# Rotary embedding of q and k as one 512-column tile, and low-order terms multiplied last, in a two-layer decoder trunk

## The chip, the cores and the metric

The kernel runs on one core of a Trainium2 chip. A core has a matrix engine (TensorE, "PE" in the profile, whose weight loads "PEld" run beside its matmuls), a vector engine (VectorE, "DVE"), a scalar engine (ScalarE, "ACT"), a general engine (GpSimd, "POOL") and a queue that issues transfers (SyncE, "SP"). The metric is the time of one execution in microseconds. Before the change it is 579.99 us, the median of three runs (579.93 to 580.3).

## The reference

The input is 256 tokens of 1024 numbers in fp32. Two layers follow one another. Layer 0 mixes tokens with 16 attention heads of 64; it is a block-sparse attention with blocks of 256 tokens, and as there are only 256 tokens, each query sees just its own block, so it is plain causal attention. Layer 1 has 12 heads in three groups, with dilated windows (128 wide with step 1, 512 with step 4, 2048 with step 16), merged over the groups by their softmax denominators. After each mixer comes a normalisation, then a squared-ReLU MLP (1024 to 4096 to 1024) and another normalisation. Cut to what matters:

```python
def apply_rotary(t, cos, sin):            # on q and on k, every head
    t1, t2 = jnp.split(t, 2, axis=-1)
    return jnp.concatenate([t1 * c - t2 * s, t2 * c + t1 * s], axis=-1)
...
x = layer_norm(alpha * x + mixer(x))      # q, k, v = x @ w_qkv; rotary; softmax(q k^T / 8) v; @ w_o
x = layer_norm(alpha * x + relu(x @ w_in) ** 2 @ w_out)
```

## The kernel before

**Numbers in two parts.** Each fp32 operand is split into a high part in a 4-byte matmul type (fp32r) and the rest: `split` makes `hi` as an ACT copy (L309) and `lo` as a DVE subtract (L314). A product is three matmul terms: hi by hi, lo by hi, hi by lo. Weights come in tiles of 128x1024: `load_w` issues one transfer of 512 KB into one of four `raw` buffers, ACT writes `whi`, DVE writes `wlo`; there are ten slots for each. `xs` holds the two parts of the layer's input with features on the partitions, in eight slices of 128 features (`kt`, 0 to 7).

**Matmuls.** Three helpers record them. `mm_wstat` (L440) has the weights stationary and makes a 128x256 tile of q or k (two heads by 256 tokens): for each `kt`, hi by hi, hi by lo part of x, lo weight by hi, 24 matmuls of 256 columns in all. `mm_xstat` (L466) has the input stationary and makes a 128-token half of V or of an MLP chunk kept in token order, 512 columns at a time, again with the three terms together for each `kt`. `mm_rows` multiplies an activation tile with a row block of an output weight (attention output or second MLP weight) into four accumulators. All matmuls go through one line, L318. PSUM has two families of banks of 128x512, four named `acc` and four named `tp`.

**Attention.** Heads are worked in pairs: eight in layer 0, six in layer 1. For a pair, `project` (or the step `qk` of layer 1) multiplies q, rotates q, multiplies k, rotates k. The feature order within a pair is laid out so that the two halves of the rotation lie 64 partitions apart. `rotate` (L511) does three DVE multiplies from PSUM with a table of cosines and sines (128x256 by cos into `a`; two of 64x256 by sin into `b`, each reading the other half's partitions), one POOL add of 128x256 (L503), and then the split into `qhi` and `qlo`, or, for k, a split twice with a mask for each head (`khi` on ACT, L529; `klo` on DVE, L508). `score` makes the scores from those, `softmax` masks (DVE, L563), takes exponentials (ACT, L573) and scales (DVE, L580); then the probabilities are transposed on PE (L587), copied out by ACT (`pt`, L595) and multiplied with V. The first four weight tiles of layer 0, two pairs, are interleaved with the loading of the input (`Stage`, `first_ps`): they have four `acc` banks, one for each of q0, k0, q1, k1.

**Seams.** At the end of a mixer or MLP, `out_and_ln` (L722) does the output products of token half 0, its normalisation (`ln_half`, L668: DVE sums and statistics, a POOL power, DVE scalings into `tok`, PE transposes of `tok`, and the split into `xs`), then those of half 1. Before the normalisation of half 1 a function `between` records the first work of the next stage that needs half 0 alone: `Mlp.head`, with `half(0)`, or layer 1's V for half 0 (`v1`). `TAIL` says how many of the last output row blocks are held back to be done bank by bank there; for layer 1's mixer it is 5 of 6. `half(m)` of the MLP makes one 512-wide chunk in token order: `mm_xstat`, then `relu_sq_tok` (ACT relu L749 and square L750 into `hrt`, four PE transposes, a split). The other seven chunks go through `mm_wstat_wide` and `relu_sq_T`.

**The order of the work.** The code above only records operations, with what they read and write, a cost and an engine. A planner (`Plan.order`) then gives each a due time, counted back from the PE operations that need it in recorded order, and builds one fixed order for each engine: at each step the operation that can start first, and of those the one with the smallest due time. PE's own due times come from the recorded order of stages, which is a string for each layer (`ORDER0`, `HEAD1`, `ORDER1`; `qk-p` projects a pair, `v` makes V, `s` is scores and softmax, `o` the product with V). SP issues the transfers in the order of recording. So a change of a recorded operation can move others on every engine.

Of the kernel before, what the change touches and what calls it, by code (L numbers as in the profile page):

```python
# [29 lines left out]
TAIL = (5, 5, 5, 8)  # L30
# [48 lines left out]
class Op:  # L79
    __slots__ = ("n", "eng", "cost", "fn", "preds", "succs", "bufs", "due", "wait", "ready", "end", "xfer", "early")  # L80


class Plan:
# [16 lines left out]
    def op(self, eng, cost, fn, reads=(), writes=(), xfer=0.0, early=0.0):  # L100
        o = Op()
        o.n, o.eng, o.cost, o.fn, o.xfer = len(self.ops), eng, cost, fn, xfer
        o.early = early
# [24 lines left out]
        self.ops.append(o)  # L128
        return o

    def order(self):
        clock = {e: BEGIN[e] for e in ("PE", "SP")}
        bus = 0.0
        for o in self.ops:
            t = max([clock.get(o.eng, 0.0)] + [p.end + latency(p, o) for p in o.preds])
            o.end = t + o.cost
            if o.eng in clock:
                clock[o.eng] = o.end
            if o.xfer:
                bus = o.end = max(t + FETCH, bus) + o.xfer  # L140
            o.due = t if o.eng == "PE" else None
# [101 lines left out]
    "bst mx sm mv rstd ta hrt raw whi wlo g b xs0 xs1 tok m1 ahi alo ropet khi klo v sc1 sc0 pt0 pt1 m0 qhi qlo ident"  # L243
# [5 lines left out]
def tile_trunk(  # L249
# [87 lines left out]
    class Stage:  # L337
# [40 lines left out]
        def mms(self, ps, j):  # L378
            kt, hi, lo = self.kt, self.hi, self.lo
            c = slice(self.col(j), self.col(j) + P)  # L380
            i = (kt, self.part(j))
            for w, p, start, stop in ((hi, 0, kt == 0, False), (hi, 1, False, False), (lo, 0, False, kt == KT - 1)):
                op(
                    "PE", 0.12,
                    lambda w=w, p=p, start=start, stop=stop: mm(
                        ps.t[:, :S], w.t[:, c], xs[kt // 4].t[:, kt % 4, p, :], start, stop
                    ),
                    [(w, i)] + [(xs[kt // 4], (p, kt, m)) for m in range(2)], [ps],
                )
# [18 lines left out]
    idle = mk([P, S], F32, "ta", 5)  # L408
    op("DVE", 0.1, lambda: nc.vector.memset(idle.t, 0.0), (), [idle])
    idle_ps = psum("tp")  # L410
    for _ in range(NWARM):
        op("PE", 0.43, lambda: mm(idle_ps.t[:, :S], idle.t[:, :P], idle.t, True, True), [idle], [idle_ps])
# [27 lines left out]
    def mm_wstat(ps, w):  # L440
        for kt in range(KT):

            def go(kt=kt):
                c = slice(kt * P, (kt + 1) * P)
                a, b = (xs[kt // 4].t[:, kt % 4, part, :] for part in range(2))
                first, last = kt == 0, kt == KT - 1
                mm(ps.t[:, :S], w.hi.t[:, c], a, first, False)
                mm(ps.t[:, :S], w.hi.t[:, c], b, False, False)
                mm(ps.t[:, :S], w.lo.t[:, c], a, False, last)

            op("PE", 0.36, go, [(w.hi, 0), (w.lo, 0)] + xk(kt, (0, 1)), [ps])
# [14 lines left out]
    def mm_xstat(ps, ws, m, n):  # L466
        t = slice(m * P, (m + 1) * P)
        for kt in range(KT):
            per = 1024 // n
            w = ws[kt // per]  # L470

            def go(kt=kt, w=w):
                c = slice((kt % per) * n, (kt % per + 1) * n)
                a, b = (xs[kt // 4].t[:, kt % 4, part, t] for part in range(2))
                mm(ps.t[:, :n], a, w.hi.t[:, c], kt == 0, False)
                mm(ps.t[:, :n], a, w.lo.t[:, c], False, False)
                mm(ps.t[:, :n], b, w.hi.t[:, c], False, kt == KT - 1)

            op("PE", 3 * (n / 2400 + 0.0135), go, [(w.hi, 0), (w.lo, 0)] + xk(kt, (m,)), [ps])
# [31 lines left out]
    def rotate(ps, kind, ropet):  # L511
        a = mk([P, S], F32, "ta", 5)
        b = mk([P, S], F32, "ta", 5)
        tt(S, lambda: a.t, lambda: ps.t[:, :S], lambda: ropet.t[:, 0, :], ALU.mult, [ps, ropet], [a],
           extra=0.1)
        tt(S, lambda: b.t[0:64, :], lambda: ps.t[64:128, :S], lambda: ropet.t[64:128, 1, :], ALU.mult,
           [ps, ropet], [(b, 0)], extra=0.1)
        tt(S, lambda: b.t[64:128, :], lambda: ps.t[0:64, :S], lambda: ropet.t[0:64, 1, :], ALU.mult,
           [ps, ropet], [(b, 1)], extra=0.1)
        tt(S, lambda: a.t, lambda: a.t, lambda: b.t, ALU.add, [a, b], [a], ADD_ENG)  # L520
        if kind == "q":
            hi, lo = mk([P, S], F32R, "qhi", 2), mk([P, S], F32R, "qlo", 2)
            split(S, lambda: a.t, lambda: hi.t, lambda: lo.t, [a], [hi], [lo], sbuf=True)
        else:
            hi, lo = mk([P, 2, S], F32R, "khi", 2), mk([P, 2, S], F32R, "klo", 2)
            for h in range(2):
                op(
                    "ACT", act(S, 1, True),
                    lambda h=h: nc.scalar.activation(hi.t[:, h, :], a.t, AF.Copy, scale=hm.t[:, h : h + 1]),  # L529
                    [a, hm], [(hi, h)],  # L530
                )
                stt(
                    S, 1, lambda h=h: lo.t[:, h, :], lambda: a.t, lambda h=h: hm.t[:, h : h + 1],
                    lambda h=h: f32(hi.t[:, h, :]), ALU.mult, ALU.subtract, [a, hm, (hi, h)], [(lo, h)],
                )
        return hi, lo

    def proj_qk(w):
        ps = psum("acc")
        mm_wstat(ps, w)  # L540
        return ps

    first_ps = [psum("acc") for _ in range(NFIRST)]
    for st in stages:
        for j, ps in enumerate(first_ps):
            st.mms(ps, j)
# [35 lines left out]
    def transposes(ps, pairs, r):  # L582
# [6 lines left out]
        op("PE", 0.109 * len(pairs), go, list(r) + [ident], [ps])  # L589
# [78 lines left out]
    def ln_half(pieces, m, gb, last):  # L668
# [21 lines left out]
        for n in range(2):  # L690
# [12 lines left out]
            if not last:  # L703
                ps = psum("tp")
                transposes(
                    ps, [(j * P, lambda k=n * 4 + j: z.t[:, k * P : (k + 1) * P]) for j in range(4)], [(z, n)]
# [15 lines left out]
    def out_and_ln(acc, items, ntail, gb, last, between):  # L722
# [4 lines left out]
        for m in range(2):  # L727
# [5 lines left out]
            ln_half(acc[m], m, gb, last)  # L733

    def relu_sq_T(ps, ahi, alo, j):
        u = mk([P, S], F32, "ta", 5)
        h = mk([P, S], F32, "ta", 5)
        keys = [(j, 0), (j, 1)]
        op("ACT", act(S), lambda: nc.scalar.activation(u.t, ps.t[:, S:], AF.Copy), [ps], [u])  # L739
        tt(S, lambda: u.t, lambda: ps.t[:, :S], lambda: u.t, ALU.add, [ps, u], [u])  # L740
        stt(S, 0, lambda: h.t, lambda: u.t, lambda: 0.0, lambda: u.t, ALU.max, ALU.mult, [u], [h])
        split(
            S, lambda: h.t, lambda: ahi.t[:, j, :], lambda: alo.t[:, j, :], [h],
# [3 lines left out]
    def relu_sq_tok(ps, m, ahi, alo):  # L747
        r = mk([P, 512], F32, "hrt", 1)
# [11 lines left out]
    class Mlp:  # L760
# [55 lines left out]
    def layer0(between):  # L816
# [3 lines left out]
        def do_v(n):  # L820
            ws = [load_w(wv0[n * 4 + j]) for j in range(4)]
            if n == 0:
                late["m0"] = const(mask0, [P, 256], "m0")
                late["ident"] = const(ident_in, [P, P], "ident")
            V[n] = []
            for m in range(2):
                ps = psum("tp" if n == m == 0 else "acc")
                mm_xstat(ps, ws, m, 512)
                V[n].append(evac_v(ps, 512))

        def softmax(q, k):
# [12 lines left out]
            m0 = late["m0"]  # L844
            for e, c, s, mc, i, n in regs:
                mask_min(
                    n, lambda e=e, c=c: e.t[:, c], lambda s=s, c=c: s.t[:, c], lambda mc=mc: m0.t[:, mc],
# [13 lines left out]
        def project(p):  # L861
            return [
                rotate(
                    first_ps[i] if i < NFIRST else proj_qk(load_w(wqk0[i - NFIRST])), kind,
                    ropes[0],
                )
                for i, kind in ((2 * p, "q"), (2 * p + 1, "k"))
            ]
# [26 lines left out]
    def v1(i, m):  # L895
# [4 lines left out]
        mm_xstat(ps, wv[i], m, v_cols[i])  # L900
# [6 lines left out]
    def layer1(between):  # L907
# [4 lines left out]
        for step, a in (x.split("-") for x in ORDER1.split()):  # L912
# [4 lines left out]
            if step == "qk":  # L917
                qk[u, gi] = [
                    rotate(proj_qk(load_w(wqk1[u * 6 + 2 * gi + i])), kind, ropes[1]) for i, kind in enumerate("qk")
                ]  # L920
# [68 lines left out]
def _layout(inputs):  # L989
# [48 lines left out]
    d["rope0"] = np.stack([np.concatenate([c] * 4), np.concatenate([s, s, -s, -s])], axis=1)  # L1038
# [48 lines left out]
```

## Time and profile before

| | value |
|---|---|
| median of 3 runs | 579.99 us (579.93 to 580.3) |
| the profiled execution | 579.34 us |
| its span in the trace | 577.2 us |
| mean granted TensorE clock | 0.996 |
| PE busy | 562.7 us, 97% |
| DVE busy | 431.3 us, 75% |
| ACT busy | 299.9 us, 52% |
| POOL busy | 36.9 us, 6% |
| transfers | 105.61 MB, mean 183 GB/s |

The span runs from the first to the last instruction that the profiler recorded; 2.1 us of the execution lie around it. The profile is of one execution, 0.65 us below the median. Rows in it have the start and length in us, the engine, the line of the kernel, the operation and the tiles written and read; in square brackets stands how long the engine was idle before, and what released it. A matmul's record is longer than its turn on the engine, since matmuls overlap; turns are read from one start to the next. Roughly, layer 0's attention lies at 0 to 110 us, its output and normalisation to 130, layer 0's MLP to 300, layer 1's V and attention to 377, its output and normalisation to 396, layer 1's MLP to 564, and the last normalisation to the end.

### The profile page before, as it was taken

The numbers are of one execution on the slowest core, as the hardware profiler recorded it, in microseconds if no ns is written. First come the engines' busy times: TensorE is split into PE (matmuls) and PEld (weight loads), VectorE is DVE, ScalarE is ACT, GpSimd is POOL, SyncE is SP. The second block draws the span as 40 slices with busy tenths as digits, with TensorE's granted clock in tenths as the row PEclk, the third lists the DMA queues.
The fourth block names the chain that finished last, engine by engine and source line by source line (L and its number), as shares of the span: only waits on it lengthen the run. The fifth ranks groups of instructions, "written<-read, shape, count | busy, mean of one in ns | idle before, by whom it ended". The sixth has DMA issues, their size and how long they took to land.

```text
span 577.2 us, 8665 instructions
## 1 busy us (share of the span) xinstructions
PE 562.7 (97%) x3234; PEld 486.2 (84%) x3234; DVE 431.3 (75%) x771; ACT 299.9 (52%) x501; POOL 36.9 (6%) x41
## 2 busy tenths in 40 slices
PE   9899999999999999999999999999999999999994
PEld 8789887778888888888887998877888888888884
DVE  6899888998875675675678699988976756756544
ACT  6585666747554555454534445744754544544400
POOL 0210131010000000000000222000000000000000
PEclk9999999999999999999999999999999999999998
DMA  8646843728877666565525424544888655655101
GB/s 322 219 148 188 292 140 99 223 83 276 274 248 279 204 196 190 178 213 184 182 75 177 186 75 127 168 148 161 281 279 258 202 185 178 204 183 183 36 1 73
DMA packets 30281, 105.61 MB, mean 183 GB/s; under 512 B 3488, under 2 KB 4256, under 8 KB 30240
## 3 DMA queue, kind: packets, MB, share of 16 engines
q1 hardware_dynamic: 30240, 105.07, 55.6%
q8 instruction: 25, 0.41, 0.3%
q14 instruction: 16, 0.13, 0.1%
HBM read 104.01 MB, written 1.05 MB: 182 GB/s over the span
## 4 chain that ended last, share of the span: by engine, by line
PE 89%; DVE 7%; ACT 2%; issue 2%; POOL 1%; DVEq 0%; POOLq 0%
PE acc L318 50%; PE tp L318 37%; PE tp L587 2%; DVE wlo L314 2%; DVE ta L501 2%; DVE tok L508 1%; POOL ta L503 1%; ACT sc L573 1%; DVE klo L508 0%; DVE sc L580 0%; DVE xs L314 0%; DVE bst L682 0%; ACT hrt L749 0%; DVE qlo L314 0%; ACT hrt L750 0%
## 5 line engine op out<-in xcount | busy, mean ns | idle before, releaser
L314 DVE TENSOR_TENSOR wlo<-raw,whi 128x1024 fp32r<-128x1024 f32 (+2 forms) x185 | 225.7, 1226 | 88.1 <-ACT whi L309 86.7
L309 ACT ACTIVATE whi<-raw 128x1024 fp32r<-128x1024 f32 (+2 forms) x184 | 191.1, 1047 | 144.3 <-PE tp L318 64.9
L318 PE MATMUL acc<-whi,ahi 128*128 128x512 f32 (+1 forms) x312 | 119.5, 383 | 0.0
L318 PE MATMUL acc<-wlo,ahi 128*128 128x512 f32 (+1 forms) x312 | 117.5, 380 | 0.0
L318 PE MATMUL tp<-xs,whi 128*128 128x512 f32 x448 | 112.0, 392 | 0.0
L318 PE MATMUL acc<-whi,alo 128*128 128x512 f32 (+1 forms) x312 | 100.5, 380 | 0.0
L318 PEld LDWEIGHTS tp<-xs,whi 128*128 128x128 f32 x448 | 81.2, 189 | 14.7
L318 PE MATMUL acc<-xs,whi 128*128 128x256 f32 x448 | 83.6, 289 | 0.0
L318 PEld LDWEIGHTS acc<-xs,whi 128*128 128x128 f32 x448 | 70.4, 194 | 2.5 <-issue 1.6
L318 PEld LDWEIGHTS acc<-whi,ahi 128*128 128x128 f32 x312 | 58.8, 188 | 11.3 <-issue 0.9
L318 PEld LDWEIGHTS acc<-wlo,ahi 128*128 128x128 f32 x312 | 58.8, 188 | 10.4
L318 PEld LDWEIGHTS acc<-whi,alo 128*128 128x128 f32 x312 | 57.1, 189 | 10.4
L318 PEld LDWEIGHTS tp<-xs,wlo 128*128 128x128 f32 x448 | 61.0, 191 | 4.2
L318 PE MATMUL tp<-xs,wlo 128*128 128x256 f32 x448 | 62.7, 283 | 0.0
L318 PE MATMUL acc<-xs,wlo 128*128 128x256 f32 x224 | 62.1, 284 | 0.0
L318 PEld LDWEIGHTS acc<-xs,wlo 128*128 128x128 f32 x224 | 42.8, 192 | 0.0
L501 DVE TENSOR_TENSOR ta<-acc,ropet 64x256 f32<-64x256 f32 (+1 forms) x84 | 35.1, 421 | 9.7 <-PE acc L318 8.6
L309 ACT ACTIVATE ahi<-ta 128x256 fp32r<-128x256 f32 x56 | 22.9, 409 | 28.5 <-DVE ta L508 28.5
L503 POOL TENSOR_TENSOR ta<-ta,ta 128x256 f32<-128x256 f32 x28 | 28.2, 1014 | 119.8 <-DVE ta L501 105.8
L688 POOL TENSOR_TENSOR rstd<-rstd,expo 128x1 f32<-128x1 f32 x8 | 7.9, 987 | 414.6 <-DVE rstd L686 414.6
L318 PE MATMUL acc<-whi,xs 128*128 128x512 f32 (+1 forms) x112 | 32.9, 364 | 0.9 <-DVE xs L314 0.6
L501 DVE TENSOR_TENSOR ta<-tp,ta 128x256 f32<-128x256 f32 x56 | 23.5, 419 | 7.9 <-ACT ta L739 7.9
(83 smaller groups left out, 548.2 us busy)
## 6 DMA issues: line engine op xcount, KB each, us to landing
raw<-in_win_dram SPq DMA_DIRECT2D x64, 512.0 KB, 4.3
raw<-in_wout_dram SPq DMA_DIRECT2D x64, 512.0 KB, 4.2
raw<-in_wqk_dram SPq DMA_DIRECT2D x24, 512.0 KB, 4.0
raw<-in_wo_dram SPq DMA_DIRECT2D x14, 512.0 KB, 3.3
raw<-in_wv_dram SPq DMA_DIRECT2D x8, 512.0 KB, 6.1
g<-in_lng_dram SPq DMA_DIRECT2D x4, 512.0 KB, 7.0
b<-in_lnb_dram SPq DMA_DIRECT2D x4, 512.0 KB, 8.0
raw<-in_wv1a_dram SPq DMA_DIRECT2D x4, 512.0 KB, 3.2
```

The source lines that it names most:

```text
L309: op("ACT", act(n, sbuf=sbuf), lambda: nc.scalar.activation(hi(), src(), AF.Copy), r, whi)
L314: lambda: nc.vector.tensor_tensor(lo(), src(), f32(hi()), op=ALU.subtract), list(r) + list(whi), wlo,
L318: nc.tensor.matmul(out_ap, lhsT, rhs, start=start, stop=stop)
L501: op("DVE", dve(n) + extra, lambda: nc.vector.tensor_tensor(out_ap(), a(), b(), op=alu), r, w)
L503: op("POOL", n / 480 + 0.17, lambda: nc.gpsimd.tensor_tensor(out_ap(), a(), b(), op=alu), r, w)
L508: lambda: nc.vector.scalar_tensor_tensor(dst(), a(), s(), b(), op0=o0, op1=o1), r, w,
L573: lambda: nc.scalar.activation(e(), e(), AF.Exp, bias=bias(), scale=-1.0, accum_out=total()), r, w,
L587: nc.tensor.transpose(ps.t[:, c : c + P], src(), ident.t)
L688: op("POOL", 0.98, lambda: nc.gpsimd.tensor_tensor(rs.t[:, 1:2], rs.t[:, 0:1], expo.t, op=ALU.pow), [(rs, 0), expo], [(rs, 1)])
```

## The change

Five edits are made together.

1. q and k of a pair are multiplied into one PSUM bank, q in columns 0 to 255 and k in 256 to 511 (for the first two pairs, two `acc` banks in place of four), and `rotate` works on the pair: ACT copies the two halves, swapped, out of PSUM into `b` (64x512 each), DVE multiplies PSUM by cos into `a` and `b` by sin in place (128x512 each), POOL adds `b` to `a` (128x512). The splits into q and k parts read `a`'s columns and are as before. q's rotation thereby starts when k's projection is done as well. The sign of the sine table's halves is exchanged, since the product is now formed after the swap.
2. In `mm_wstat` all hi-weight terms of the eight slices come before the lo-weight terms. In `mm_xstat` one term of each slice is moved behind all others: the one with x's lo part (`late` "x": the MLP's halves and layer 1's V) or the one with the weight's lo part (`late` "w": layer 0's V). The number of matmuls is the same.
3. `TAIL` for layer 1's mixer is 6 in place of 5: all six row blocks are done bank by bank.
4. A PE operation can be given an earlier due time (`ahead`); the transposes of token half 1's normalisation get 1.5 where a next stage follows.
5. Scratch: five `ta` tiles of 128x256 become four of 128x512, `relu_sq_T` uses the two halves of one, `hrt` becomes a `ta`, and layer 0's mask uses layer 1's tile.

```diff
-TAIL = (5, 5, 5, 8)
+TAIL = (5, 5, 6, 8)
...
-            o.due = t if o.eng == "PE" else None
+            o.due = t - o.ahead if o.eng == "PE" else None
...
-    def mm_wstat(ps, w):
+    def mm_wstat(ps, w, c0):
+        def go_hi(kt):
+            for part in range(2):
+                mm(ps.t[:, c0 : c0 + S], w.hi.t[:, kt * P : (kt + 1) * P], xs[kt // 4].t[:, kt % 4, part, :], kt + part == 0, False)
+        def go_lo(kt):
+            mm(ps.t[:, c0 : c0 + S], w.lo.t[:, kt * P : (kt + 1) * P], xs[kt // 4].t[:, kt % 4, 0, :], False, kt == KT - 1)
         for kt in range(KT):
-            def go(kt=kt):
...
-            op("PE", 0.36, go, [(w.hi, 0), (w.lo, 0)] + xk(kt, (0, 1)), [ps])
+            op("PE", 0.24, lambda kt=kt: go_hi(kt), [(w.hi, 0)] + xk(kt, (0, 1)), [ps])
+        for kt in range(KT):
+            op("PE", 0.12, lambda kt=kt: go_lo(kt), [(w.lo, 0)] + xk(kt, (0, 1)), [ps])
...
-    def mm_xstat(ps, ws, m, n):
+    def mm_xstat(ps, ws, m, n, late):
...
+        third = (1, 0) if late == "x" else (0, 1)
+        for terms, first, last in ((((0, 0), third[::-1]), True, False), ((third,), False, True)):
+            for kt in range(KT):
...
-    def rotate(ps, kind, ropet):
-        a = mk([P, S], F32, "ta", 5)
-        b = mk([P, S], F32, "ta", 5)
-        tt(S, lambda: a.t, lambda: ps.t[:, :S], lambda: ropet.t[:, 0, :], ALU.mult, [ps, ropet], [a],
-           extra=0.1)
-        tt(S, lambda: b.t[0:64, :], lambda: ps.t[64:128, :S], lambda: ropet.t[64:128, 1, :], ALU.mult,
-           [ps, ropet], [(b, 0)], extra=0.1)
-        tt(S, lambda: b.t[64:128, :], lambda: ps.t[0:64, :S], lambda: ropet.t[0:64, 1, :], ALU.mult,
-           [ps, ropet], [(b, 1)], extra=0.1)
-        tt(S, lambda: a.t, lambda: a.t, lambda: b.t, ALU.add, [a, b], [a], ADD_ENG)
+    def rotate(ps, ropet):
+        a = mk([P, 512], F32, "ta", 4)
+        b = mk([P, 512], F32, "ta", 4)
...
+        for h in range(2):
+            op(
+                "ACT", act(512) + 0.1,
+                lambda h=h: nc.scalar.activation(b.t[64 * h : 64 * h + 64, :], ps.t[64 - 64 * h : 128 - 64 * h, :], AF.Copy),
+                [ps], [(b, h)],
+            )
+        tt(512, lambda: pair(a.t), lambda: pair(ps.t), lambda: table(0), ALU.mult, [ps, ropet], [a])
+        tt(512, lambda: pair(b.t), lambda: pair(b.t), lambda: table(1), ALU.mult, [b, ropet], [b])
+        tt(512, lambda: a.t, lambda: a.t, lambda: b.t, ALU.add, [a, b], [a], ADD_ENG)
...
-    first_ps = [psum("acc") for _ in range(NFIRST)]
+    first_ps = [psum("acc") for _ in range(NFIRST // 2)]
...
-            ln_half(acc[m], m, gb, last)
+            ln_half(acc[m], m, gb, last, 1.5 if m == 1 and between else 0.0)
...
     def relu_sq_T(ps, ahi, alo, j):
-        u = mk([P, S], F32, "ta", 5)
-        h = mk([P, S], F32, "ta", 5)
+        both = mk([P, 512], F32, "ta", 4)
...
     def relu_sq_tok(ps, m, ahi, alo):
-        r = mk([P, 512], F32, "hrt", 1)
+        r = mk([P, 512], F32, "ta", 4)
...
-                mm_xstat(ps[c], self.ws[c], m, 512)
+                mm_xstat(ps[c], self.ws[c], m, 512, "x")
...
-                mm_xstat(ps, ws, m, 512)
+                mm_xstat(ps, ws, m, 512, "w")
...
-            return [
-                rotate(
-                    first_ps[i] if i < NFIRST else proj_qk(load_w(wqk0[i - NFIRST])), kind,
-                    ropes[0],
-                )
-                for i, kind in ((2 * p, "q"), (2 * p + 1, "k"))
-            ]
+            if 2 * p < NFIRST:
+                return rotate(first_ps[p], ropes[0])
+            return rotate(proj_qk([load_w(wqk0[2 * p + i - NFIRST]) for i in range(2)]), ropes[0])
...
-        mm_xstat(ps, wv[i], m, v_cols[i])
+        mm_xstat(ps, wv[i], m, v_cols[i], "x")
```

More of the change, by code (lines that the diff above doesn't have):

```diff
@@ L79 @@
 class Op:
-    __slots__ = ("n", "eng", "cost", "fn", "preds", "succs", "bufs", "due", "wait", "ready", "end", "xfer", "early")
+    __slots__ = ("n", "eng", "cost", "fn", "preds", "succs", "bufs", "due", "wait", "ready", "end", "xfer", "early", "ahead")
 class Plan:
@@ L242 @@
 LAYOUT = (
-    "bst mx sm mv rstd ta hrt raw whi wlo g b xs0 xs1 tok m1 ahi alo ropet khi klo v sc1 sc0 pt0 pt1 m0 qhi qlo ident"
+    "bst mx sm mv rstd ta raw whi wlo g b xs0 xs1 tok m1 ahi alo ropet khi klo v sc1 sc0 pt0 pt1 qhi qlo ident"
 ).split()
@@ L381, in mms @@
             i = (kt, self.part(j))
-            for w, p, start, stop in ((hi, 0, kt == 0, False), (hi, 1, False, False), (lo, 0, False, kt == KT - 1)):
+            last = kt == KT - 1 and j % 2 == 1
+            for w, p, start, stop in ((hi, 0, kt == 0 and j % 2 == 0, False), (hi, 1, False, False), (lo, 0, False, last)):
                 op(
@@ L538, in proj_qk, with pair, table @@
-    def proj_qk(w):
+    def rotate(ps, ropet):
+        a = mk([P, 512], F32, "ta", 4)
+        b = mk([P, 512], F32, "ta", 4)
+        def pair(ap):
+            return ap.rearrange("p (i s) -> p i s", i=2)
+        def table(i):
+            return ropet.t[:, i, :].unsqueeze(1).to_broadcast([P, 2, S])
+        for h in range(2):
+            op(
+                "ACT", act(512) + 0.1,
+                lambda h=h: nc.scalar.activation(b.t[64 * h : 64 * h + 64, :], ps.t[64 - 64 * h : 128 - 64 * h, :], AF.Copy),
+                [ps], [(b, h)],
+            )
+        tt(512, lambda: pair(a.t), lambda: pair(ps.t), lambda: table(0), ALU.mult, [ps, ropet], [a])
+        tt(512, lambda: pair(b.t), lambda: pair(b.t), lambda: table(1), ALU.mult, [b, ropet], [b])
+        tt(512, lambda: a.t, lambda: a.t, lambda: b.t, ALU.add, [a, b], [a], ADD_ENG)
+        q = mk([P, S], F32R, "qhi", 2), mk([P, S], F32R, "qlo", 2)
+        split(S, lambda: a.t[:, :S], lambda: q[0].t, lambda: q[1].t, [a], [q[0]], [q[1]], sbuf=True)
+        hi, lo = mk([P, 2, S], F32R, "khi", 2), mk([P, 2, S], F32R, "klo", 2)
+        for h in range(2):
+            op(
+                "ACT", act(S, 1, True),
+                lambda h=h: nc.scalar.activation(hi.t[:, h, :], a.t[:, S:], AF.Copy, scale=hm.t[:, h : h + 1]),
+                [a, hm], [(hi, h)],
+            )
+            stt(
+                S, 1, lambda h=h: lo.t[:, h, :], lambda: a.t[:, S:], lambda h=h: hm.t[:, h : h + 1],
+                lambda h=h: f32(hi.t[:, h, :]), ALU.mult, ALU.subtract, [a, hm, (hi, h)], [(lo, h)],
+            )
+        return q, (hi, lo)
@@ L587, in go @@
                 nc.tensor.transpose(ps.t[:, c : c + P], src(), ident.t)
-        op("PE", 0.109 * len(pairs), go, list(r) + [ident], [ps])
+        op("PE", 0.109 * len(pairs), go, list(r) + [ident], [ps], ahead=ahead)
     halves = (slice(0, P), slice(P, S))
@@ L666, in act_tiles, with ln_half @@
         return mk([P, 4, S], F32R, "ahi", 3), mk([P, 4, S], F32R, "alo", 3)
[L668 removed]
+    def ln_half(pieces, m, gb, last, ahead):
         g, b = gb
```

93 lines of the change are left out of this document (41 added, 52 removed).

## The prediction

> **What bounds the kernel now.** I read the page first: the engines' totals, the chain that ended last, the group this change replaces.
>
> ```profile
> PE 562.7 (97%) x3234; PEld 486.2 (84%) x3234; DVE 431.3 (75%) x771; ACT 299.9 (52%) x501; POOL 36.9 (6%) x41
> ...
> PE 89%; DVE 7%; ACT 2%; issue 2%; POOL 1%; DVEq 0%; POOLq 0%
> ...
> L501 DVE TENSOR_TENSOR ta<-acc,ropet 64x256 f32<-64x256 f32 (+1 forms) x84 | 35.1, 421 | 9.7 <-PE acc L318 8.6
> ...
> L503 POOL TENSOR_TENSOR ta<-ta,ta 128x256 f32<-128x256 f32 x28 | 28.2, 1014 | 119.8 <-DVE ta L501 105.8
> ```
>
> TensorE is busy for 562.7 of 577.2 us, so an edit that leaves its matmuls alone, as this one does, can win no more than the time PE stands still. Next comes the table of stretches (length; busy PE, PEld, DVE, ACT, POOL; clock; DMA share; GB/s): two of layer 0's attention, layer 0's MLP, layer 1's attention, and its end with the LN behind it. Then the list of what PE waited for: total, times, longest.
>
> ```profile
> 17.40:40.20 22.80, 21.08 (x123) 18.01 (x124) 22.31 (x48) 13.84 (x29) 5.08 (x5) 1.00 0.58 185
> 40.20:76.00 35.80, 35.75 (x247) 31.77 (x248) 32.97 (x87) 24.13 (x59) 5.31 (x6) 1.00 0.62 207
> ...
> 138.40:299.80 161.40, 161.40 (x818) 137.79 (x817) 108.92 (x155) 79.74 (x117) 0.99 (x1) 1.00 0.64 208
> ...
> 327.50:377.00 49.50, 49.45 (x384) 44.93 (x382) 47.38 (x119) 29.41 (x57) 10.01 (x10) 1.00 0.41 128
> 377.00:404.40 27.40, 26.61 (x131) 21.56 (x127) 22.82 (x33) 13.34 (x18) 1.98 (x2) 1.00 0.45 150
> ```
>
> ```profile
> PE tp L318 <- DVE wlo L314: 1.6, 1, 1.6
> PE tp L587 <- ACT hrt L750: 1.5, 2, 0.8
> PE tp L318 <- DVE warm L402: 1.2, 1, 1.2
> PE tp L587 <- ACT pt L595: 1.2, 1, 1.2
> PE acc L318 <- DVE xs L314: 0.6, 1, 0.6
> PE tp L318 <- ACT pt L595: 0.5, 1, 0.5
> PE acc L318 <- ACT xs L309: 0.3, 1, 0.3
> ```
>
> Without the start's 1.2 (warm) this is 5.7 us, and it splits in two: waits at the seams of stages (1.6, 1.5, 0.6, 0.3, together 4.0) and in attention (1.2 and 0.5, together 1.7). The MLP stretch has none. In 327.5 to 377 PE is full while DVE has 2.1 us left of 49.5: there DVE works just ahead of PE, and a microsecond saved on it returns nothing unless PE has been waiting.
>
> **The change part by part.**
>
> *Rotation, DVE and ACT.* Each of 14 pairs loses six DVE multiplies (84 x 421 ns is 35.1 us) and gets two of 128x512. The nearest rows for those, and for the two new 512-column copies on ACT:
>
> ```profile
> L314 DVE TENSOR_TENSOR xs<-tp,xs 128x512 fp32r<-128x512 f32 x12 | 7.9, 683 | 0.2 <-ACT xs L309 0.2
> L662 ACT ACTIVATE v<-acc 128x512 f32<-128x512 f32 x5 | 2.9, 590 | 1.8 <-PE acc L318 1.8
> ```
>
> DVE: 6 x 0.42 = 2.5 becomes 2 x 0.68 = 1.4, 1.2 us less a pair, 16 in all. ACT: 2 x 0.59 = 1.2 more a pair, 16.5 in all, on an engine that is half idle. Off the path both are worth 0 to PE. On it, the most they return is attention's 1.7.
>
> *Rotation, order.* q's rotation now starts when k's projection is in too, 24 matmuls later (eight slices by three terms). The projections' matmuls start 0.12 apart:
>
> ```profile
> 13.24 0.28 PE L318 MATMUL acc<-xs,whi 128*128 128x256 f32 x1
> 13.36 0.28 PE L318 MATMUL acc<-xs,wlo 128*128 128x256 f32 x1
> ```
>
> That makes 2.9 us. PE does not feel it so long as the scores of a pair come later than that. The planner puts other work between: for the first pair, V's 48 matmuls. For later pairs I find margins from under 1 to several us by walking the changed order with these rows, so this term is 0 with a bound of +1.5 at single spots.
>
> *Rotation, POOL.* 28 adds of 256 columns become 14 of 512. What one costs depends on its neighbour on DVE:
>
> ```profile
> 38.21 0.73 POOL L503 TENSOR_TENSOR ta<-ta,ta 128x256 f32<-128x256 f32 x1 [8.99 <-DVE ta L501]
> ```
>
> ```profile
> 326.82 1.23 DVE L314 TENSOR_TENSOR wlo<-raw,whi 128x1024 fp32r<-128x1024 f32 x1
> ...
> 329.63 1.76 DVE L314 TENSOR_TENSOR wlo<-raw,whi 128x1024 fp32r<-128x1024 f32 x1
> ```
>
> ```profile
> 326.94 1.71 POOL L503 TENSOR_TENSOR ta<-ta,ta 128x256 f32<-128x256 f32 x1 [2.78 <-DVE ta L501]
> 329.39 0.91 POOL L503 TENSOR_TENSOR ta<-ta,ta 128x256 f32<-128x256 f32 x1 [0.76 <-DVE ta L501]
> ```
>
> Alone an add takes 0.73. Started 0.12 after a `wlo` subtract it takes 1.71; started 0.24 before one it takes 0.91 and the subtract 1.76. The two take turns. The wide add lies between 0.73 and 2 x 0.73 = 1.46 alone; I take 1.4, since the elements double. Met by a subtract it is later by 1.71 - 0.73 = 0.98, up to 2 x 1.71 = 3.4 in all. In the changed order the instruction that releases the add is the second multiply, and a `wlo` often stands right behind it on DVE: more adds will meet one. ACT's khi and qhi wait for the add, DVE's klo and qlo for those, the scores for all. I take 0 for the sum, since the rotation is ready early wherever PE was full before, and keep the 0.98 for a rival.
>
> [...]
>
> *Start.* V's first product waits for its lo part:
>
> ```profile
> 13.66 1.06 ACT L309 ACTIVATE whi<-raw 128x1024 fp32r<-128x1024 f32 x1 [0.98 <-DMA raw<-in_wv_dram]
> ...
> 16.08 1.32 DVE L501 TENSOR_TENSOR ta<-acc,ropet 128x256 f32<-128x256 f32 x3 [2.65 <-PE acc L318]
> ...
> 16.60 0.39 PE L318 MATMUL tp<-whi,xs 128*128 128x512 f32 x1
> 17.31 1.21 DVE L314 TENSOR_TENSOR wlo<-raw,whi 128x1024 fp32r<-128x1024 f32 x1
> 18.55 0.33 SPq L305 DMA_DIRECT2D raw<-in_wqk_dram  x1
> ...
> 18.58 0.50 PE L318 MATMUL tp<-wlo,xs 128*128 128x512 f32 x1 [1.59 <-DVE wlo L314]
> ```
>
> Before, V's first hi part is made at 13.66, as its data land. In the changed order a swap copy stands ahead of it on ACT, and that copy needs the whole first pair, in PSUM at about 16.45. So hi is ready at 16.45 + 0.5 + 1.06 = 18.0, and PE, with nothing else, waits from 16.6 to 18.0: 1.4. Then lo is not needed before all hi terms, half a dozen us later. A matmul of 512 columns takes twice the 0.12 of one of 256, about 0.23, so before PE lost 18.58 - 16.60 - 0.23 = 1.75. Term -0.35; bounds -1.6 (the copy costs nothing) and 0. The weights' buffers come free under 1 us later too, and SP's next load (18.55 before) with them; its data are used some 10 us on, so 0.
>
> *Seams.* The rows around the three LN boundaries:
>
> ```profile
> 128.17 1.04 PE L587 MATMUL tp<-ident,tok 128*128 128x128 f32 x8
> ...
> 128.87 0.59 ACT L309 ACTIVATE xs<-tp 128x512 fp32r<-128x512 f32 x1
> 129.34 0.63 ACT L750 ACTIVATE hrt<-hrt 128x512 f32<-128x512 f32 x1
> ...
> 130.03 0.66 PE L587 MATMUL tp<-ident,hrt 128*128 128x128 f32 x4 [0.82 <-ACT hrt L750]
> ```
>
> ```profile
> 306.36 1.41 DVE L508 SCALAR_TENSOR_TENSOR tok<-tok,rstd,b 128x512 f32<-128x512 f32 x2
> ...
> 308.05 1.03 PE L587 MATMUL tp<-ident,tok 128*128 128x128 f32 x8
> ...
> 309.38 0.50 PE L318 MATMUL acc<-whi,xs 128*128 128x512 f32 x1 [0.30 <-ACT xs L309]
> ...
> 310.70 0.74 PE L318 MATMUL acc<-whi,xs 128*128 128x512 f32 x2 [0.58 <-DVE xs L314]
> ```
>
> ```profile
> 396.05 0.66 PE L587 MATMUL tp<-ident,hrt 128*128 128x128 f32 x4 [0.66 <-ACT hrt L750]
> ```
>
> At 130 and 396 PE transposes the token half, then must wait for ACT's square. Changed, four matmuls of the next half (hi terms alone, x_lo being last) stand in between: 4 x 0.23 = 0.9 of cover, but they wait themselves for ACT's xs (done at 129.46; the eight transposes leave PE at about 129.1): 0.4. Terms -0.35 (of 0.82) and, with x_lo's lateness gone too, -0.6 (bound -0.66 and the small gaps near it); 0 at the other end. At 308 the transposes move ahead of the last four V matmuls, and V's copy behind xs; DVE's scale ends at 307.77, so PE may wait 0.3 once, in place of 0.3 and 0.58 plus their handovers (309.38 and 310.70 lie 1.2 later than back to back). Term -0.9, bounds 0 and -1.2.
>
> *The rest* (all of layer 1's output projection in the tail, shared tiles, the sign table) moves no instruction count; the final LN that ends the span is as before. 0, with the seam at 377 to 404 as its cover.
>
> Sum: -0.35 - 0.35 - 0.9 - 0.6 = -2.2. The profiled execution took 579.34, 2.1 of it around its span and 0.65 less than the median, so 577.1 there and 577.8 against 579.99.
>
> **The rivals.** *Slower: POOL and DVE take turns on the path.* Place: the add of a pair that meets a `wlo`. For it: the rows at 326 to 330, and DVE's full stretch. Against: 35.75 of 35.80 busy in the second stretch, with six adds in it that were disturbed as well (5.31 us of POOL, 0.88 each). Price 0.98 a hit that reaches PE; the third hit turns the -2.2 over. With five of 14 pairs, 4.9 - 2.2 = +2.7: 582.7. [...]
>
> *Freed DVE removes attention's waits as well.* For it: both (1.2, 0.5) end on ACT's pt behind the softmax on DVE. Against: ACT, the engine named, gets longer. 577.8 - 1.7 = 576.1.
>
> *Waits change place, nothing more*: the seams' chains (transposes, ACT, DVE) are as long as before, and covered matmuls are missing elsewhere. 580.0.
>
> **How the numbers follow.** Chances: forecast 0.43, turns on the path 0.29, waits exchanged 0.15, freed DVE 0.13. The forecast's own range is 576.1 (attention's 1.7 too) to 579.3 (one spot's 1.5). The whole range goes from 574.3, all 4.0 of seams and 1.7 gone, rounded to 574, to 583.7, six hits on the path (5.9 - 2.2 = +3.7). About 0.2%, 1.2 us, is what a measurement of this kernel can tell from none. Faster takes the forecast but a tenth that falls within the bound, and the freed DVE: 0.53; same 0.19; slower 0.28.
>
> **What would show it.** Right: four fewer DVE multiplies a pair, DVE about 415 us; PE's wait near 16.6 is 1.4 and for whi or its copy; no wait for xs lo near 309; the waits for ACT's square under 0.5. Wrong: wide adds of over 2.5 us with scores waiting for klo or qlo; a new PE wait after a projection in 40 to 76 or 327 to 377, where there was none; a busy PE total other than 562.7.

## The result, and the profile after

The change made the kernel slower: 581.64 us, the median of seven runs (581.58 to 582.49), against 579.95 for the kernel before (seven runs, 579.65 to 580.3). The ratio is 1.0031, with a 95% interval of 1.002 to 1.0043. The forecast was 577.8; the sign was wrong. The profiled execution took 581.64 too, with a span of 579.9, 2.7 us longer than the 577.2 of before.

The page of the changed kernel, its engines, the groups of the weights' lo parts and of the wide add:

```profile
PE 564.8 (97%) x3234; PEld 487.3 (84%) x3234; DVE 419.6 (72%) x715; ACT 314.3 (54%) x529; POOL 31.0 (5%) x27
...
L314 DVE TENSOR_TENSOR wlo<-raw,whi 128x1024 fp32r<-128x1024 f32 (+2 forms) x185 | 231.6, 1261 | 86.9 <-ACT whi L309 85.8
...
L515 POOL TENSOR_TENSOR ta<-ta,ta 128x512 f32<-128x512 f32 x14 | 22.3, 1594 | 134.4 <-DVE ta L513 134.4
```

DVE is busy 11.7 us less and ACT 14.4 more, much as the change sets out. But DVE's `wlo` subtracts, which the change does not touch, went from 225.7 us (1226 ns) to 231.6 (1261 ns); this is their line of before:

```profile
L314 DVE TENSOR_TENSOR wlo<-raw,whi 128x1024 fp32r<-128x1024 f32 (+2 forms) x185 | 225.7, 1226 | 88.1 <-ACT whi L309 86.7
```

The list of what PE waited for:

```profile
PE tp L608 <- DVE mx L584: 1.7, 1, 1.7
PE tp L318 <- DVE warm L403: 1.2, 1, 1.2
PE tp L318 <- ACT whi L309: 1.0, 1, 1.0
PE tp L608 <- ACT pt L616: 0.9, 1, 0.9
PE tp L318 <- ACT qhi L309: 0.8, 1, 0.8
PE tp L318 <- DVE klo L520: 0.7, 3, 0.2
PE tp L318 <- ACT xs L309: 0.6, 2, 0.3
PE tp L318 <- ACT pt L616: 0.4, 1, 0.4
```

The waits of before at the start (wlo, 1.6) and the seams (hrt 1.5, xs 0.6 and 0.3) have become 1.0 (whi) and 0.6 (xs, twice 0.3). New are 1.7 behind a mask's maximum (mx), 0.8 for qhi and 0.7 for klo: the scores now wait for the rotation. Stretches of the changed kernel, columns as before:

```profile
40.20:76.00 35.80, 34.12 (x233) 30.03 (x234) 31.14 (x69) 27.98 (x61) 4.74 (x3) 1.00 0.70 235
...
299.80:327.50 27.70, 27.70 (x178) 25.10 (x177) 18.90 (x27) 13.85 (x20) 2.28 (x2) 1.00 0.51 171
```

```profile
327.50:377.00 49.50, 47.10 (x345) 42.20 (x344) 46.48 (x102) 35.71 (x65) 8.16 (x5) 1.00 0.48 159
```

The stretch around layer 1's V has no idle PE any more (26.82 of 27.70 before). The two that were full are not: 35.75 of 35.80 became 34.12, and 49.45 of 49.50 became 47.10. Where, is seen in PE's rows that wait:

```profile
62.47 0.73 PE L608 MATMUL tp<-ident,sc 128*128 128x128 f32 x5 [1.68 <-DVE mx L584]
```

```profile
333.91 0.38 PE L318 MATMUL tp<-klo,qhi 128*128 128x256 f32 x1 [0.23 <-DVE klo L520]
341.29 0.38 PE L318 MATMUL tp<-klo,qhi 128*128 128x256 f32 x1 [0.24 <-DVE klo L520]
```

```profile
348.92 0.50 PE L318 MATMUL tp<-khi,qhi 128*128 128x512 f32 x1 [0.80 <-ACT qhi L309]
349.61 0.50 PE L318 MATMUL tp<-klo,qhi 128*128 128x512 f32 x1 [0.19 <-DVE klo L520]
354.35 0.66 PE L608 MATMUL tp<-ident,sc 128*128 128x128 f32 x4 [0.86 <-ACT pt L616]
```

The brackets count from the end of the matmul before; read from start to start, less the regular turn, each is 0.15 to 0.3 more. So read, the five rows of layer 1's attention hold 3.3 us, and with the smaller gaps beside them it is about 4; before, no gap there was over 0.21. (The expectations below speak of these 4.0 to 4.2.) One pair's rotation, from ACT's first copy to the last split, in the timeline of the changed kernel:

```profile
327.02 0.59 ACT L537 ACTIVATE ta<-acc 64x512 f32<-64x512 f32 x1
327.65 0.69 DVE L513 TENSOR_TENSOR ta<-acc,ropet 128x512 f32<-128x512 f32 x1 [1.05 <-ACT ta L537]
328.38 0.59 ACT L537 ACTIVATE ta<-acc 64x512 f32<-64x512 f32 x1 [0.76 <-DVE ta L513]
...
329.00 0.69 DVE L513 TENSOR_TENSOR ta<-ta,ropet 128x512 f32<-128x512 f32 x1 [0.66 <-ACT ta L537]
329.61 3.45 DVE L314 TENSOR_TENSOR wlo<-raw,whi 128x1024 fp32r<-128x1024 f32 x2
329.83 2.14 POOL L515 TENSOR_TENSOR ta<-ta,ta 128x512 f32<-128x512 f32 x1 [5.04 <-DVE ta L513]
```

```profile
332.01 0.91 ACT L549 ACTIVATE khi<-ta,hm 128x256 fp32r<-128x256 f32 x2 [1.01 <-POOL ta L515]
...
332.98 0.87 DVE L520 SCALAR_TENSOR_TENSOR klo<-ta,hm,khi 128x256 fp32r<-128x256 f32 x2
...
333.78 0.41 DVE L314 TENSOR_TENSOR qlo<-ta,qhi 128x256 fp32r<-128x256 f32 x1
```

Two things stand in these rows. First, ACT and DVE take turns: copy, multiply, copy, multiply, each waiting for the other, 1.98 us before the second multiply starts. The copies and the multiply by cos share no written tile; what they share is the PSUM bank that they read. In none of the 14 pairs does a copy overlap a multiply of its bank; the planner, for which two reads are free, does not count that. Second, the add starts 0.2 after a subtract, and takes 2.14 where one that finds no subtract running takes 1.29; and the two subtracts take 3.45 where two take 2.35. So the add waits for the first, and holds up the second, which takes 2.32 in place of 1.22. An add that starts ahead of a subtract holds it up as well: twelve of the 180 full-width subtracts took 1.5 to 2.35 us, the others about 1.2.

Summed over the kernel, the lists of DVE's and of ACT's waits:

```profile
DVE ta L513 <- ACT ta L537: 14.5, 13, 4.2
```

```profile
ACT ta L537 <- DVE ta L513: 8.4, 9, 1.8
```

Not all of DVE's 14.5 us is due to the turns: 9.8 of it lies at three pairs (17.50, 77.35 and 321.32) whose first copy had itself waited for PE's projection.

These rows alone do not show that the shared bank is what makes them take turns; the run below in which the multiply does not read it tests that.

### The profile page after: what moved, and what is told of

It is laid out like the page before. It is cut to its first block, busy times and chain, and to the rows that moved or that the text cites. A ratio compares the mean times of both kernels' runs of the same rounds, so it can differ in the third digit from the quotient of the medians.

```text
span 579.9 us, 8599 instructions
## 1 busy us (share of the span) xinstructions
PE 564.8 (97%) x3234; PEld 487.3 (84%) x3234; DVE 419.6 (72%) x715; ACT 314.3 (54%) x529; POOL 31.0 (5%) x27
## 4 chain that ended last, share of the span: by engine, by line
PE 82%; DVE 8%; ACT 6%; issue 2%; DMA 1%; POOL 0%; SPq 0%; DVEq 0%; ACTq 0%; POOLq 0%
PE acc L318 45%; PE tp L318 35%; DVE wlo L314 3%; PE tp L608 2%; ACT ta L537 2%; ACT whi L309 2%; DVE ta L513 2%; DVE klo L520 1%; ACT sc L594 1%; DMA raw<-in_xw_dram 1%; DVE sc L584 1%; DVE qlo L314 0%; DVE tok L520 0%; DVE sc L601 0%; ACT pt L616 0%
## 5 line engine op out<-in xcount | busy, mean ns | idle before, releaser
L314 DVE TENSOR_TENSOR wlo<-raw,whi 128x1024 fp32r<-128x1024 f32 (+2 forms) x185 | 231.6, 1261 | 86.9 <-ACT whi L309 85.8
L318 PE MATMUL acc<-xs,whi 128*128 128x256 f32 x448 | 65.1, 288 | 0.0
L318 PEld LDWEIGHTS acc<-xs,whi 128*128 128x128 f32 x448 | 59.1, 194 | 2.1 <-issue 1.1
L318 PE MATMUL acc<-xs,wlo 128*128 128x256 f32 x224 | 36.5, 287 | 0.0
L318 PEld LDWEIGHTS acc<-xs,wlo 128*128 128x128 f32 x224 | 31.4, 194 | 0.5 <-issue 0.3
L515 POOL TENSOR_TENSOR ta<-ta,ta 128x512 f32<-128x512 f32 x14 | 22.3, 1594 | 134.4 <-DVE ta L513 134.4
L318 PE MATMUL acc<-whi,xs 128*128 128x512 f32 (+1 forms) x112 | 28.7, 363 | 0.0
L314 DVE TENSOR_TENSOR alo<-ta,ahi 128x256 fp32r<-128x256 f32 x56 | 23.3, 419 | 6.3 <-ACT ahi L309 6.3
```

The lines of the kernel that those rows point to most:

```text
L314: lambda: nc.vector.tensor_tensor(lo(), src(), f32(hi()), op=ALU.subtract), list(r) + list(whi), wlo,
L318: nc.tensor.matmul(out_ap, lhsT, rhs, start=start, stop=stop)
L515: op("POOL", n / 480 + 0.17, lambda: nc.gpsimd.tensor_tensor(out_ap(), a(), b(), op=alu), r, w)
```

## The experiments

Theory B: ACT's copies and DVE's multiply take turns at the bank that they both read, and the loss comes from that. Theory P: it comes from POOL's wide add, which DVE's subtracts hold up and which holds them up. The order that the planner makes is a third thing, since an edit of a recorded operation can move it. Behind each group of expectations stand the measured times in the same order, with the ratio to the kernel before, measured beside it, and its 95% interval.

**Which part loses.** One run has the kernel before with the late terms, `ahead` and `TAIL`, and its own rotation; another has the new rotation alone.

```diff
 # e1_seams: the kernel before, with mm_wstat, mm_xstat, ahead and TAIL of the changed one
 # e2_rot: the changed kernel, with the order of terms of the kernel before, and
-TAIL = (5, 5, 6, 8)
+TAIL = (5, 5, 5, 8)
-            ln_half(acc[m], m, gb, last, 1.5 if m == 1 and between else 0.0)
+            ln_half(acc[m], m, gb, last, 0.0)
```

> The kernel before with the late terms, the earlier due time and the tail of 6, and its own rotation (q and k apart, three multiplies each on DVE). If the loss is the rotation's alone, the gains at the start and the seams stay, about 0.6 + 0.5 + 1.2 + 0.8 = 3.1, and the time is 576.5 to 577.3. If the late terms and due times themselves disturb the attention stages, it is 579 or more.

> The kernel before with the new rotation alone (one bank for a pair, copies on ACT, two wide multiplies, one wide add) and its scratch; terms, due times and tail as before. If the rotation makes the loss: new waits of PE in both attention stages, some 4 to 5 us in all, 583.5 to 585. If the loss comes from the two halves of the change meeting, 580 to 581.

Measured: 577.41 us, ratio 0.9959 (0.9942 to 0.9975), and 583.29, ratio 1.0058 (1.0043 to 1.0073). The first is faster by 2.5 and the second slower by 3.4, and the sum, +0.9, is within 0.8 of the whole change's +1.7. The loss is the rotation's.

**POOL's add taken over by DVE; ACT's copies taken over by DVE.**

```diff
 # e3_add_on_dve
-ADD_ENG = "POOL"
+ADD_ENG = "DVE"
 # e4_no_copies: no ACT copies, the multiply by cos recorded first (and the sine table's signs as before)
-        tt(512, lambda: pair(b.t), lambda: pair(b.t), lambda: table(1), ALU.mult, [b, ropet], [b])
+        for h in range(2):
+            dst, src = slice(64 * h, 64 * h + 64), slice(64 - 64 * h, 128 - 64 * h)
+            tt(512, lambda dst=dst: pair(b.t[dst, :]), lambda src=src: pair(ps.t[src, :]), ...)
```

> The changed kernel with the wide add on DVE in place of POOL. [...]

> The changed kernel without ACT's copies: DVE multiplies the swapped halves by sin straight from PSUM (two of 64x512), so DVE alone reads the bank. DVE has 0.7 more a pair, POOL's wide add stays. Theory B: no turns between ACT and DVE, DVE's 14.5 us of waiting for the copies goes, PE's waits in layer 1 fall below 2 us: 578.5 to 580. Theory P: the adds meet subtracts as before, 581.5 to 582.5.

Measured: 577.51 (0.9957; 0.9941 to 0.9974) and 580.88 (1.0019; 1.0007 to 1.0032). Of the first P asked 578 to 579, with the add at 0.7 on every pair and never held up, and B 581 to 582: it speaks for P. The second lies between B's numbers and P's and decides nothing: the turns are gone (no copies, and so none of the 14.5 us), but DVE has one more multiply of 0.69 on each pair, 9.7 us in all, and PE still stands in both attention stages.

**The planner told of the bank.** DVE's multiply by cos is given the copies' tile as a read, so it comes after both in the plan; b's scratch tile has to be taken first for that.

```diff
 # e5_planner_knows_bank (e8_bank_and_dve_add: and ADD_ENG = "DVE")
-        a = mk([P, 512], F32, "ta", 4)
         b = mk([P, 512], F32, "ta", 4)
+        a = mk([P, 512], F32, "ta", 4)
-        tt(512, lambda: pair(a.t), lambda: pair(ps.t), lambda: table(0), ALU.mult, [ps, ropet], [a])
+        tt(512, lambda: pair(a.t), lambda: pair(ps.t), lambda: table(0), ALU.mult, [ps, ropet, b], [a])
 # e6_two_adds: POOL's add in columns 256:512 and then 0:256
 # e7_planner_add_2p1
-            op("POOL", n / 480 + 0.17, ...)
+            op("POOL", 2.1, ...)
```

> [...] Theory B (turns at the bank, unknown to the planner): the idle of DVE before the multiplies falls well below 14.5 us and PE's waits in layer 1's attention by 2 or more: 579 to 580. Theory P (POOL's wide add, its length and its turns with DVE's subtracts): within 0.7 of the changed kernel, 581 to 582.3.

> The changed kernel with POOL's add in two of 256 columns, k's first. If the length of the one add is what is late, k's parts start 0.55 earlier on each of 14 pairs and about 1 to 1.5 us of waits go: 580 to 580.7. If the turns with DVE's subtracts are (each of two adds may meet one), nothing is won: 581.3 to 582.5.

> The changed kernel with the planner told that an add on POOL takes 2.1 us (what it takes when it meets a subtract) in place of 1.24. The work is the same, only the order may move. If the add is late because the order has no room for it, the planner now makes some and the waits for klo and qhi fall: 578.5 to 580. If the lateness is a chain that no order hides, or the turns come at other places in its stead, 581 to 583.

> Both: the planner knows that the multiply follows the copies, and DVE adds. Against the 577.5 of the add on DVE alone: theory B has 1 to 2 us more to win, 575.5 to 576.5; theory P none, 577 to 578.

Measured: 575.46 (0.9917; 0.9902 to 0.9932), 581.58 (1.0022; 1.0013 to 1.0032), 580.32 (1.0002; 0.9993 to 1.0011) and 574.91 (0.9911; 0.9897 to 0.9926). One dependency, with all of the work as in the changed kernel, won 6.2 us, more than B had asked for. DVE's wait and the stretch of layer 1's attention in that run:

```profile
DVE ta L513 <- ACT ta L537: 6.6, 2, 4.2
```

```profile
327.50:377.00 49.50, 49.39 (x373) 44.33 (x373) 43.70 (x103) 36.93 (x70) 7.63 (x5) 1.00 0.49 165
```

DVE waits for the copies twice in place of 13 times, and PE is full again. POOL's adds are met by subtracts at least as often there (its mean add is 1662 ns, against 1594). But the subtracts themselves take 225.7 us in that run, 5.9 less than in the changed kernel: the new order also lets the adds hold up DVE less, so the 6.2 is not the bank's alone. Splitting the add won nothing; a larger cost for it in the plan won 1.3, less than the 1.6 to 3.1 asked for. The run with both cures, 574.91 us, computes everything and is about 1% under both kernels; it cannot be told from the 575.46 of the one dependency, so with the dependency known the add on DVE won nothing clear.

**Is it only the order?** Three more: the tiles' order alone; the opposite dependency (multiply first, then both copies); and the dependency in the run with the new rotation alone.

```diff
 # e9_scratch_order: b's mk ahead of a's, nothing else
 # e10_multiply_first: the multiply recorded ahead of the copies, and
-                [ps], [(b, h)],
+                [ps, a], [(b, h)],
 # e11_rotation_known: e2_rot with the edit of e5_planner_knows_bank
```

> Of the two edits in the run in which the planner knows the bank, the lesser one alone: b's scratch tile is taken before a's, so that the planner may place the copies before the multiply; the order of multiply and copies at the bank stays unknown to it. If the knowledge is what won the 6 us, this is like the changed kernel, 580 to 582; if the tiles' order did, 575 to 576.5.

> The changed kernel with the opposite dependency given to the planner: DVE's multiply by cos first, then both copies. If it is enough that the planner knows the turns, 575.5 to 578; if the win was the copies coming first, 580 or more.

> The kernel before with the new rotation alone, now with the dependency (copies, then multiply) known to the planner; terms, due times and tail as before. If the turns at the bank were all that was wrong with the rotation, its 583.3 falls by as much as the changed kernel's did: 577 to 578.5. If the rotation is a loss in itself and only the late terms make up for it, 580 or more.

Measured: 583.45 (1.0061; 1.0046 to 1.0076), 577.37 (0.9952; 0.9935 to 0.9969) and 581.68 (1.0029; 1.0018 to 1.004). Knowing the turns wins either way round, by 6.2 and 4.3, and the tiles' order does not. But the tiles' order alone cost 1.8 us with no change of work, so an order by itself is worth some 2 us. And the third run came out on the side of a loss in the rotation itself: without the late terms the known dependency won 1.6 and not 5. An argument from runs with different orders was not enough.

**The order held fixed.** In these four, each engine's instructions stand in the order of the changed kernel, and their traces have them in that order; only what one instruction touches is another, so each leaves out a part of the rotation's result.

```diff
 # e12_same_order_no_turns: the multiply by cos reads the table, not the bank
-        tt(512, lambda: pair(a.t), lambda: pair(ps.t), lambda: table(0), ALU.mult, [ps, ropet], [a])
+        tt(512, lambda: pair(a.t), lambda: table(0), lambda: table(0), ALU.mult, [ps, ropet], [a])
 # e13_same_order_short_add: 32 columns are added (e14_same_order_neither: both edits)
-        tt(512, lambda: a.t, lambda: a.t, lambda: b.t, ALU.add, [a, b], [a], ADD_ENG)
+        tt(512, lambda: a.t[:, :32], lambda: a.t[:, :32], lambda: b.t[:, :32], ALU.add, [a, b], [a], ADD_ENG)
 # e15_same_order_long_no_port: ahead of the short add, in the same step on POOL
+            nc.gpsimd.memset(b.t[:, 32:], 0.0)
+            nc.gpsimd.memset(b.t[:, 32:], 0.0)
```

> The changed kernel with every engine's order kept as it is; only DVE's multiply by cos reads the table in place of q and k, so it doesn't touch the PSUM bank and neither waits for ACT's copies nor they for it (the cosine term is thereby left out of q and k). If the turns at the bank are the loss, the waits of PE in layer 1's attention fall from 4.2 to 2 or less and the time to 578 to 579.5. If they only made the planner's order unlucky, or POOL's add is the loss, 581 or more.

> The changed kernel, order kept on every engine; POOL adds 32 of the 512 columns (the sine term is left out of the others), so the add's length and its turns with DVE's subtracts go and the turns at the bank stay. If the add is the loss, 1.0 us on each pair and 1.9 on the five that are met come off the rotation: 578 to 579.5. If the bank is: 580.5 to 581.6.

> Both of these left out, order kept. If the two together carry the loss in the attention stages (layer 1's 4.0 and the 1.8 at 62), it goes: 576 to 577.5. If the order itself is at fault, 579 or more.

> As the run with the short add, order kept; but ahead of the add of 32 columns POOL writes zeros over the rest of b twice (480 columns each), so POOL's part of the chain is long again, by writes that read nothing from SBUF (the sine term is left out of those columns). If it is the length of POOL's part that costs, the time goes back towards 581.6 in proportion to the length these writes turn out to have; if it is that the add holds up DVE's next subtract, it stays at 577 to 578.

Measured: 577.6 (0.9957; 0.9942 to 0.9972), 577.01 (0.9946; 0.9928 to 0.9964), 573.9 (0.9895; 0.9879 to 0.9912) and 576.14 (0.9932; 0.9914 to 0.995). Against the 581.64 of the changed kernel it is worth 4.0 that the multiply does not read the bank, 4.6 that the add is short, and 7.7 that both are so, a little under the sum. In the first, ACT's 8.4 us of waits for the multiply are gone, copies and multiplies overlap (the multiply at 54.92 starts 0.24 after the copy at 54.68), and the subtracts take as long as in the changed kernel (231.4 us). Its multiply does not wait for the projection either; what of the 4.0 comes from that is not separated. DVE's wait in the first of them, and the stretch of layer 1's attention without either:

```profile
DVE ta L513 <- ACT ta L537: 6.9, 4, 3.6
```

```profile
327.50:377.00 49.50, 49.50 (x375) 44.81 (x374) 41.59 (x105) 35.67 (x67) 1.87 (x4) 1.00 0.52 171
```

The fourth tells what it is about the add. Its rows at one pair, POOL and then DVE, and below them the changed kernel's rows for the same pair:

```profile
57.05 0.50 POOL L543 MEMSET ta<- 128x480 f32 x1 [6.34 <-DVE ta L513]
57.61 0.50 POOL L544 MEMSET ta<- 128x480 f32 x1
58.07 1.30 POOL L545 TENSOR_TENSOR ta<-ta,ta 128x32 f32<-128x32 f32 x1
```

```profile
56.91 2.35 DVE L314 TENSOR_TENSOR wlo<-raw,whi 128x1024 fp32r<-128x1024 f32 x2
```

```profile
57.28 2.14 POOL L515 TENSOR_TENSOR ta<-ta,ta 128x512 f32<-128x512 f32 x1 [6.79 <-DVE ta L513]
```

```profile
57.05 3.45 DVE L314 TENSOR_TENSOR wlo<-raw,whi 128x1024 fp32r<-128x1024 f32 x2
```

POOL's part is 2.3 us long here (57.05 to 59.37, the short add being held up by the second subtract, 1.30 in place of 0.25), longer than the 2.14 it replaces. Over the 14 pairs POOL is busy for 25.9 us with the writes and the short adds, where the wide adds took 22.3, and the time stays at 576.1. So its length is not what costs. What is gone is the 1.1 us for which DVE's second subtract stood still: 3.45 became 2.35. Over the kernel the group of subtracts shows it, of the run with the short add:

```profile
L314 DVE TENSOR_TENSOR wlo<-raw,whi 128x1024 fp32r<-128x1024 f32 (+2 forms) x185 | 221.4, 1206 | 87.2 <-ACT whi L309 86.9
```

Against 231.6 in the changed kernel, the wide adds took 10.2 us of DVE's time; by the same measure the narrow adds of before took about 4.3 (225.7). Across different orders this sum does not give the time. In the run with two narrower adds the subtracts took 226.8 us, and nothing was won. With the add on DVE they took 221.7, but the 14 adds cost DVE 9.7 us in their place (0.69 each), and still 4.1 were won. Why, is not shown. In the rows above the writes of 0.50, which read no tile, run beside a subtract and neither is longer: the 28 writes took 0.50 each on the mean, and the two subtracts 2.35. What in the add holds up a subtract was not taken apart further.

## Why the prediction was wrong

**Start: right.** It had PE wait 1.4 for whi in place of 1.75 for wlo, -0.35. The row at 18.46 of the changed kernel waits for whi, and start to start PE loses 1.2: -0.55.

```profile
18.46 0.74 PE L318 MATMUL tp<-whi,xs 128*128 128x512 f32 x2 [1.03 <-ACT whi L309]
```

**Seams: right.** Forecast -0.35, -0.9 and -0.6. The square's waits at 130 and 396 are gone, the token half's first matmul waits 0.30 for xs there, and around 308 nothing waits:

```profile
130.27 0.50 PE L318 MATMUL tp<-whi,xs 128*128 128x512 f32 x1 [0.30 <-ACT xs L309]
```

```profile
398.61 0.50 PE L318 MATMUL tp<-whi,xs 128*128 128x512 f32 x1 [0.30 <-ACT xs L309]
```

Read from start to start these are -0.5, -1.2 and -0.8, with the start -3.05 where -2.2 was forecast; the run with these edits alone, 2.5 faster, bears the sum out.

**"Rotation, DVE and ACT", taken as 0: this step failed first.** It set ACT's copies and DVE's multiplies side by side, each by its own row, and called both off the path. They read one bank and take turns: in none of the 14 pairs do they overlap. For the pair shown that is copy, multiply, copy, multiply in a row. ACT stood 8.4 us for DVE's multiplies, and of DVE's 14.5 us behind the copies 6.9 were left when the multiply did not read the bank; with the order held 4.0 us of the time hang on it. I had priced instructions and not looked at what each waits for.

**"Rotation, POOL", taken as 0: this step failed too.** Its rows were the right ones. The wide add took 1.29 alone, inside the stated 0.73 to 1.46, and 2.14 when met, on five of 14 pairs (9 x 1.29 + 5 x 2.14 = 22.3, the group's total), which is the rival's count. But the sum asked only how late the add is. The quoted row in which a subtract took 1.76 in place of 1.23 was the one that counted: the add's time comes off DVE's queue. It is worth 4.6 with the order held. The argument that hits miss the path was misread as well: of the six adds in 40 to 76, said to be disturbed, one took 1.72 and the five others 0.73 to 0.75.

The 4.0 and 4.6 are what it is worth to take each away. They are not shares of the 3.8 us by which the forecast was missed: the narrow adds of before took DVE's time too, and with both gone the time, 573.9, is 3.9 under the forecast.

**"Rotation, order", 0 with a bound of 1.5 at single spots:** the margins were walked with a chain that lacked both of these. For the pair above it takes 7.2 us from the first copy to the last split (327.02 to 334.19), and the scores were there first. Two of the stated signs of being wrong came: new waits behind a projection (0.80 at 348.92), and PE's busy total, 564.8 in place of 562.7 with the same 3234 matmuls. A record outlasts its turn (0.28 against 0.12 in the rows of the projection), so short gaps lie inside it; from start to start PE's gaps of over 0.05 us sum to 24.7 against 22.5.

**DVE's total** was to be 415; it is 419.6. The 5.9 us by which the subtracts grew are more than the difference.

**The rivals.** The slower one named POOL and DVE taking turns, with 582.7 for five hits; 581.64 came, with five adds met. That the number is so near is partly luck: the mechanism is about half of what the two are worth, and its price was the add's lateness, which the run with POOL's part long again shows to cost nothing in this order. "Freed DVE removes attention's waits" failed: DVE was freed by 11.7 us of work, but its waits ahead of the rotation's multiplies went from 8.6 us (for PE) to 15.1 (14.5 for the copies). With both cures, though, the new rotation is 2.5 us faster than the old one with the same late terms (574.91 against 577.41, in different orders). The bank was on nobody's list. In the chances, 0.53 and 0.28 should be 0.52 and 0.29 by the rule given there.

**What stays open.** Why the rotation alone, with the bank known, is still 1.7 slower than before (581.68), when the same edit took the whole change 4.5 under it. Its trace has waits of PE at other places than the changed kernel's: from start to start 2.1 at 48 us behind `pt`, 1.2 behind klo in layer 1, and at the start 1.2 for whi and 1.0 more for wlo, where before had 1.76 in all. Whether the late terms are what gives the rotation room, or the planner's order fell badly, was not tried. The add on DVE won 4.1 in one order and not clearly anything in another. And the two terms of 4.0 and 4.6 hold for this one order.

## What to carry to other kernels

Before an instruction is moved to a second engine, ask what both engines then touch: here ACT's copies and DVE's multiplies of one PSUM bank ran at once in none of the 14 pairs, and a scheduler that counts reads as free placed them side by side and left the queues behind them late. An operation given to POOL was not free for DVE here: 14 adds that were 22.3 us of POOL took 10.2 us from DVE's subtracts. To tell a cause from the luck of a list scheduler, keep every engine's order and change only what one instruction touches.

## What the runs showed of the hardware that was not expected

- POOL's add by width, with no subtract running as it starts: 0.25 us for 32 columns, 0.73 for 256, 1.29 for 512. Started behind a running subtract, the one of 512 took 2.14, and the subtract queued behind it on DVE about 2.3 in place of 1.2. POOL's write of 480 columns took 0.50 beside a subtract that kept its length.
- An order alone, with the same instructions (b's scratch tile taken before a's), moved the time from 581.64 to 583.45.
